# A hybrid decoder layer: interleaved output projection, grouped down product, weight loads issued from GpSimd

## The chip, the cores and the metric

The kernel runs on one core of one Trainium2 chip. The metric is the device time of one execution in microseconds, the median of several runs. Smaller is better. The engines are called as the profile calls them: PE (TensorE), DVE (VectorE), ACT (ScalarE), POOL (GpSimd), SP (SyncE, which only issues transfers here).

## The reference

One layer for 1024 prompt tokens and 8 x 8 decode tokens, 1088 in all, model width 1024, MLP width 4096. Two mixers (retention, and sliding-window attention with sinks) read one projection of the normed input; `concatenate([o_r, o_s])` below is their result. The part that the change touches starts behind them:

```python
    h = x + jnp.concatenate([o_r, o_s], axis=-1) @ w_out
    hf = rms_norm(h, norm_ffn_gain)
    h = h + jnp.square(jax.nn.relu(hf @ w_up)) @ w_down
    return h, new_ret, new_k, new_v
```

## The kernel before

All large products are fp32 in three passes: each operand is split into a rounded high part and the rest, and `mm3` issues high x high, low x high, high x low. A split (`halve`) is an ACT cast for the high part and a subtraction on DVE or POOL for the low part (`lo`).

The 1088 tokens are two halves s = 0, 1 of 544, each in two column blocks h of Q = 272. The stages follow each other:

- **Front**: input projection, retention and attention. Their results go to DRAM (`mr_hi_d` and so on) and come back as `mixa` (attention) and `mixr` (retention) for one half s at a time (`mix_load`).
- **Output projection**, `out_proj(s, m)` for eight blocks m of 128 output rows, 48 matmuls each. It loads and splits the block of w_out (`wo`), multiplies it by mixa and mixr, adds the residual x (`y`), stores the sum to DRAM (`y_d`), and keeps it times the norm's gain in `f` and its squares in `acc`. Half 0 is interleaved with the last retention blocks; half 1 follows with the eight PSUM banks of `psM`.
- **Operands**: up and down use a scheme with seven products instead of eight for a 2 x 2 block product. `operands(s, m)` forms the seven right-hand operands (`op0` to `op6`) as differences of `f` on POOL, and splits them (casts on ACT, `lo` on DVE).
- **Norm**, `norm(s)`: column sums of `acc` on PE (`psr`), scaling on DVE, a power on POOL (`rsqrt_inplace`), and then two transfers to DRAM and a broadcast load back give the factor `rsf` on all partitions. norm(0) is issued after m = 1 of half 1, norm(1) inside the first block of up.
- **Up**, 16 blocks `up(fp)`: the left operands `wu` are w_up's four quarters and three combinations of them that POOL adds up (`left`, `comb`), in the order PROD = (1, 2, 6, 5, 7, 4, 3), 48 / 2 = 24 matmuls each over both halves. The results are rectified, scaled by `rsf`, squared (`m`, `v`, `r`, `rt`), turned into the next product's operands by differences on POOL (`rt`) and stored to DRAM (`u_d`).
- **Down**, eight groups of two blocks of w_down: for each of seven products i the two blocks' left operands (`wd..a`, `wd..b`) and the stored operands (`ur`, split into `uh` and `ul`) are multiplied into eight PSUM banks (`psd`), and each bank is added to an accumulator `a` in SBUF. The stored y (`yt`) is added during groups 1 to 6.

Tile pools hand out buffers; whoever needs one waits until its last reader is done (`wa`, `wb`: four split weights each; `raw`: three raw weight halves). A scheduler decides the order of the instructions on each engine ahead of time, and every engine works its own list in order. All data transfers are issued from SP's list. `psM` and all of the last stages' buffers belong to the last four stages, so each stage's first loads wait for buffers of the one before.

## Time and profile before

| | |
|---|---|
| median of 3 runs | 1321.57 us (1320.02 to 1322.45) |
| the profiled execution | 1318.76 us, span 1317.0 us |
| busy share of the span | PE 93%, DVE 64%, POOL 53%, ACT 38% |
| mean granted TensorE clock | 0.966 |
| front and half 0 of the output projection | to about 518 us |
| half 1 | 518 to 598 us |
| up | 598 to 953 us |
| down | 953 to 1317 us |

A row of groups reads: line, engine, operation, written tile <- read tiles, shape, count, then busy time and the mean of one in ns, then the idle time of the engine before them and what ended it. A row of PE's waits reads: the waiting matmul, what it waited for, total us, how often, the longest. A row of a window gives for each engine its busy time and the number of instructions, then the granted clock (1.00 is full speed).

### The profile page before, as it was taken

Reading aid. Unit: us, or ns where it says so; the run is one execution under the profiler, and the core shown is the slowest. Engines: PE = TensorE matmul, PEld = TensorE weight load, DVE = VectorE, ACT = ScalarE, POOL = GpSimd, SP = SyncE. Lnnn points to the kernel's source line nnn. Section 1 sums busy time; section 2 is a strip of 40 time slices with the busy share of each in tenths; the row PEclk is TensorE's granted clock in tenths of the full one; section 3 lists DMA queues with packets and bytes.
Section 4 is the critical chain, followed back from the end, with each engine's and each line's share of the span. In section 5 each row is a group of like instructions: output and inputs, shape, how many; then the busy total and the mean of one; then the engine's idle time right before and its main releaser. Section 6 shows DMA issues by size and latency. Waiting matters only on the chain.

```text
span 1317.0 us, 24166 instructions
## 1 busy us (share of the span) xinstructions
PE 1227.8 (93%) x9581; PEld 1161.9 (88%) x9581; DVE 842.5 (64%) x1549; ACT 504.5 (38%) x1027; POOL 696.0 (53%) x542
## 2 busy tenths in 40 slices
PE   7989999999998698595999999999959999999998
PEld 5979877778978698595999999999959999999998
DVE  8736645543136567486666666767455888888886
ACT  5333334354213324153444344444444333333331
POOL 8325232222324423225566666656685887789761
PEclk9989999999999899698999999999989999999999
DMA  6211223324405855562243424243544445545434
GB/s 222 66 55 56 76 78 96 114 79 127 124 35 183 283 185 166 117 186 71 108 152 124 171 105 183 93 183 112 202 159 142 154 157 178 167 153 157 142 103 170
DMA packets 112778, 178.96 MB, mean 136 GB/s; under 512 B 14048, under 2 KB 82592, under 8 KB 112408
## 3 DMA queue, kind: packets, MB, share of 16 engines
q1 hardware_dynamic: 112663, 177.41, 41.1%
q8 instruction: 75, 1.23, 0.4%
q14 instruction: 40, 0.32, 0.1%
HBM read 119.31 MB, written 58.07 MB: 135 GB/s over the span
## 4 chain that ended last, share of the span: by engine, by line
PE 77%; DMA 8%; DVE 7%; POOL 5%; issue 1%; ACT 1%; SPq 0%; DVEq 0%; ACTq 0%; POOLq 0%
PE psd L181 7%; PE psd L179 7%; PE psd L180 7%; PE psx L179 5%; PE psx L181 5%; PE psx L180 5%; PE psf L181 3%; PE psf L179 3%; PE psf L180 3%; PE psz L181 2%; PE psz L179 2%; PE psz L180 2%; PE pst L179 2%; PE pst L180 2%; PE pst L181 2%; PE po L421 2%
## 5 line engine op out<-in xcount | busy, mean ns | idle before, releaser
L1045 DVE TENSOR_TENSOR a<-a,psd 128x272 f32<-128x272 f32 x416 | 162.4, 429 | 43.8 <-PE psd L181 43.3
L755 DVE TENSOR_TENSOR ul<-ur,uh 128x1088 fp32r<-128x1088 f32 (+1 forms) x57 | 108.5, 1908 | 25.9 <-ACT uh L754 23.7
L367 POOL TENSOR_TENSOR sp<-sp,ssp 128x1024 f32<-128x1024 f32 (+1 forms) x16 | 28.6, 1787 | 110.0 <-DVE ssp L366 110.0
L179 PE MATMUL psx<-op_1h,wu_w 128*128 128x272 f32 x256 | 75.0, 293 | 7.1 <-ACT m L974 7.1
L755 DVE TENSOR_TENSOR wu_w<-wu_s,wu_w 128x512 fp32r<-128x512 f32 x64 | 69.9, 1093 | 15.9 <-ACT wu_w L754 14.7
L179 PE MATMUL psx<-op_0h,wu_w 128*128 128x272 f32 x256 | 74.9, 292 | 0.0
L181 PE MATMUL psx<-op_1l,wu_w 128*128 128x272 f32 x256 | 74.7, 292 | 0.0
L181 PE MATMUL psx<-op_0l,wu_w 128*128 128x272 f32 x256 | 74.5, 291 | 0.0
L180 PE MATMUL psx<-op_1h,wu_w 128*128 128x272 f32 x256 | 74.3, 290 | 0.0
L180 PE MATMUL psx<-op_0h,wu_w 128*128 128x272 f32 x256 | 74.1, 289 | 0.0
L961 DVE SCALAR_TENSOR_TENSOR m<-m,rsf 128x272 f32<-128x272 f32 x96 | 61.8, 644 | 11.9 <-DMA rsf<-r_d 9.2
L754 ACT CAST uh<-ur 128x1088 fp32r<-128x1088 f32 (+1 forms) x57 | 61.8, 1087 | 9.0 <-PE psd L180 9.0
L181 PE MATMUL psf<-hnl,wqk_hi 128*128 128x384 f32 (+1 forms) x192 | 65.0, 339 | 0.0
L995 POOL TENSOR_TENSOR rt<-rt 128x272 f32<-128x272 f32 x64 | 64.3, 1014 | 1.2
L179 PE MATMUL psf<-hnh,wqk_hi 128*128 128x384 f32 (+1 forms) x192 | 64.9, 338 | 0.0
L180 PE MATMUL psf<-hnh,wqk_lo 128*128 128x384 f32 (+1 forms) x192 | 64.8, 338 | 0.0
L995 POOL TENSOR_TENSOR rt<-r,rt 128x272 f32<-128x272 f32 x32 | 31.7, 992 | 62.0 <-ACT r L962 62.0
L755 DVE TENSOR_TENSOR wu_w<-wu_r,wu_w 128x512 fp32r<-128x512 f32 x48 | 41.6, 868 | 27.5 <-ACT wu_w L754 27.5
L179 PEld LDWEIGHTS psx<-op_1h,wu_w 128*128 128x128 f32 x256 | 48.8, 191 | 7.3 <-ACT m L974 7.3
L956 DVE TENSOR_TENSOR m<-m,psz 128x272 f32<-128x272 f32 x64 | 28.0, 437 | 41.5 <-ACT m L974 26.6
L754 ACT CAST wu_w<-wu_s 128x512 fp32r<-128x512 f32 x64 | 39.8, 622 | 37.4 <-PE psy L181 30.5
L403 DVE SCALAR_TENSOR_TENSOR sp<-dtab,nsl,scp 128x256 f32<-128x256 f32 (+1 forms) x64 | 28.5, 459 | 37.4 <-PE scp L402 37.0
(511 smaller groups left out, 4902.8 us busy)
## 6 DMA issues: line engine op xcount, KB each, us to landing
u_d<-rt SPq DMA_DIRECT2D x32, 952.0 KB, 5.7
ur<-u_d SPq DMA_DIRECT2D x56, 544.0 KB, 4.0
wu_r<-in_w_up SPq DMA_DIRECT2D x32, 512.0 KB, 4.2
wo_raw<-in_w_out SPq DMA_DIRECT2D x16, 512.0 KB, 4.1
y<-in_xY SPq DMA_DIRECT2D x16, 272.0 KB, 3.0
y_d<-y SPq DMA_DIRECT2D x16, 272.0 KB, 2.4
yt<-y_d SPq DMA_DIRECT2D x16, 272.0 KB, 3.6
out_yT<-a SPq DMA_DIRECT2D x16, 272.0 KB, 2.2
```

What stands on the lines that cost most here:

```text
L179: nc.tensor.matmul(ps, lh, rh, start=first, stop=False, skip_group_check=more)
L180: nc.tensor.matmul(ps, ll, rh, start=False, stop=False, skip_group_check=more)
L181: nc.tensor.matmul(ps, lh, rl, start=False, stop=last, skip_group_check=more)
L367: nc.gpsimd.tensor_tensor(s, s, ss.unsqueeze(2).broadcast_to([P, 4, n]), ALU.mult)
L403: nc.vector.scalar_tensor_tensor(s[:, g, :], dtab[:, 256 - n :], nsl[:, c, kv, g : g + 1], pg, ALU.mult, ALU.add)
L421: nc.tensor.matmul(po[p_, :], vs[:, c - 1 + h, p_], pts[kv][:, h, :], start=h == halves[0], stop=h == 1)
L754: nc.scalar.copy(hi, src)
L755: lo_eng.tensor_tensor(lo, src, hi.bitcast(F32), ALU.subtract)
L956: nc.vector.tensor_tensor(t_, t_, bank_, ALU.add)
L961: nc.vector.scalar_tensor_tensor(t_, src, 0.0, rsf[:, s, h, :], ALU.max, ALU.mult)
L995: sub = lambda o_, p_, q_: nc.gpsimd.tensor_tensor(o_, p_, q_, ALU.subtract)
L1045: nc.vector.tensor_tensor(to, to, ps, ALU.add)
```

## The change

Four things are done, all behind the front:

1. **Output projection.** Each block is split into an `a` half (mixa) and an `r` half (mixr), and w_out is loaded as pairs of such halves. In half 1 the `a` halves of m = 0 to 3 come first, the `r` halves after them, then pairs m = 4, 5 and 6, 7. In half 0 the split weights are made one block ahead. `operands(0, ...)` are interleaved with half 1. The squares get a tile of their own.
2. **Norm.** The factors no longer pass through DRAM: PE broadcasts them with matmuls against the identity (`psn`), and ACT copies them into `rsf`. norm(0) moves behind m = 2, 3. The first two products' weights of up are split while the output projection ends.
3. **Down.** Five groups of 2, 4, 4, 4 and 2 blocks instead of eight of 2, so that fewer banks are emptied (448 become 280, 32 of them by ACT as before); the `lo` subtraction of `wd` moves from POOL to DVE. The y additions stand in groups 1 and 2.
4. **Transfers.** The raw loads of w_up and w_down, the loads of y and the stores `y_d` are issued from GpSimd.

```diff
     def rawload(src, name, tag="raw", pl=None):
-        raw = (pl or mw).tile([P, 1024], F32, tag=tag, name=name, bufs=3)
-        nc.sync.dma_start(raw, src)
+        raw = (pl or mw).tile([P, 1024], F32, tag=tag, name=name, bufs=9 if tag == "rawb" else 3)
+        nc.gpsimd.dma_start(raw, src)
         return raw
...
+    def wo_pair(s, m, half):
+
+        raw = mw.tile([P, 1024], F32, tag="raw", name=f"wo{half}{s}_{m}_raw", bufs=3)
+        c0 = 512 * (half == "a")
+        nc.sync.dma_start(
+            raw.rearrange("p (m n) -> p m n", m=2), a["w_out"][m : m + 2, :, c0 : c0 + 512].rearrange("m p n -> p m n")
+        )
+        for i in range(2):
+            yield wsplit(raw[:, i * 512 : i * 512 + 512], "wa", f"wo{half}{s}_{m + i}", nc.vector)
+
+    def out_half(s, half, ps, h, w, first, last):
+        for k in range(4):
+            lh, ll = (w[:, i, k * 128 : k * 128 + 128] for i in range(2))
+            mh, ml = (mix[s, half + x][:, k, h, :] for x in "hl")
+            mm3(ps, lh, ll, mh, ml, first and k == 0, last and k == 3)
+
+    def residual(s, m, pss):
         y = om.tile([P, 2, Q], F32, tag="y", name=f"y{s}_{m}", bufs=2)
-        nc.sync.dma_start(y.rearrange("p h n -> p (h n)"), a["xY"][:, s, m, :])
+        nc.gpsimd.dma_start(y.rearrange("p h n -> p (h n)"), a["xY"][:, s, m, :])
         for h in range(2):
...
-            nc.vector.tensor_tensor(y[:, h, :], ps, y[:, h, :], ALU.add)
+            nc.vector.tensor_tensor(y[:, h, :], pss[h], y[:, h, :], ALU.add)
         kk, k2 = m % 4, m // 4
-        nc.sync.dma_start(y_d[:, 2 * k2 : 2 * k2 + 2, kk, s, :], y)
+        nc.gpsimd.dma_start(y_d[:, 2 * k2 : 2 * k2 + 2, kk, s, :], y)
...
+    def out_parts(s, ms, half, psum, pss):
+
+        for m in ms:
+            if m % 2 == 0:
+                gen = wo_pair(s, m, half)
+            w = next(gen)
+            for h in range(2):
+                if half == "a":
+                    pss[m, h] = psum()
+                out_half(s, half, pss[m, h], h, w, half == "a", half == "r")
...
-        nc.vector.tensor_scalar(rf, ps[:, :5], 1.0 / 1024.0, EPS, ALU.mult, ALU.add)
-        rsqrt_inplace(rf, 5)
-        c0 = 2 * Q * s
-        nc.sync.dma_start(r_d[c0 : c0 + 512].rearrange("(t p) -> p t", p=128), rf[:, :4])
-        nc.sync.dma_start(r_d[c0 + 512 : c0 + 544].rearrange("(p t) -> p t", t=1), rf[96:128, 4:5])
-        nc.sync.dma_start(
-            rsf[:, s, :, :].rearrange("p h n -> p (h n)"), r_d[c0 : c0 + 544].unsqueeze(0).broadcast_to([P, 544])
-        )
...
+        nc.vector.tensor_scalar(rf, ps[:, :6], 1.0 / 1024.0, EPS, ALU.mult, ALU.add)
+        rsqrt_inplace(rf, 6)
+        for h in range(2):
+            pb = psM.tile([P, 512], F32, tag="b", name=f"psn{s}{h}")
+            for i, (c0, n) in enumerate(((0, 128), (128, 128), (256, 16))):
+                nc.tensor.matmul(
+                    pb[:, c0 : c0 + n], rf[:, 3 * h + i : 3 * h + i + 1].broadcast_to([P, 128]), ident[:, 128 - n :],
+                    start=True, stop=True,
+                )
+            nc.scalar.copy(rsf[:, s, h, :], pb[:, :Q])
...
+    out_parts(1, range(4), "a", late, pss)
+    for m in (2, 6, 3, 7):
+        operands(0, m)
+    mx0x.close()
+    operand_tiles(1)
+    mix_load(1, "r", ox.enter_context(pool("mxR", side="right")))
+    rest = [0, 4, 1, 5]
+    for ms in ((0, 1), (2, 3), (4, 5), (6, 7)):
+        if ms[0] > 3:
+            out_parts(1, ms, "a", late, pss)
+        out_parts(1, ms, "r", late, pss)
+        if ms == (6, 7):
+            gen0 = left(PROD, a["w_up"][0], "wu0", nc.vector, tags=("wa", "wa", "wb", "wb"))
+            ready = [next(gen0), next(gen0)]
+        for m in ms:
+            residual(1, m, [pss[m, h] for h in range(2)])
+            if rest:
+                operands(0, rest.pop(0))
+            operands(1, m)
+        if ms == (2, 3):
+            norm(0)
...
-    for g in range(8):
-        gens = [
-            left(DOWN, a["w_down"][2 * g + 1], f"wd{g}b", nc.gpsimd, "rawb", dn, "Sb", dn, ("wb",)),
-            left(DOWN, a["w_down"][2 * g], f"wd{g}a", nc.gpsimd, tags=("wa",)),
-        ]
+    for g, (f0, nf) in enumerate(((0, 2), (2, 4), (6, 4), (10, 4), (14, 2))):
+        gens = []
+        for f in range(nf):
+            own = ("rawb", dn, "Sb", dn) if f else ("raw", mw, "S", mid)
+            gens.append(left(DOWN, a["w_down"][f0 + f], f"wd{f0 + f}", nc.vector, *own, tags=("wb" if f % 2 else "wa",)))
```

How the lists of the engines move is shown at three places. The first is DVE at the end of half 0. Before, from the last block's weights on (`wo1_1` is block 1 of half 1, `op0_0l` a low part of half 0's operands; runs of such rows are cut short here):

```order
L755 TENSOR_TENSOR wo1_0_1_5398<-wo1_0_raw_5393,wo1_0_1_5398 128x512 [waits Activation_49]
L788 TENSOR_TENSOR y0_7_5213<-pso_5215,y0_7_5213 128x272 [waits DMAHW6_49,PE_49]
L802 TENSOR_TENSOR acc0_4589<-acc0_4589,y0_6_5146 128x544 [waits Activation_49]
L788 TENSOR_TENSOR y0_7_5213<-pso_5241,y0_7_5213 128x272 [waits PE_49]
L755 TENSOR_TENSOR op3_0l_5289<-f0_1_4654,op3_0h_5288 128x272 [waits Activation_49]
L755 TENSOR_TENSOR wo1_1_0_5467<-wo1_1_raw_5465,wo1_1_0_5467 128x512 [waits Activation_49]
L755 TENSOR_TENSOR op3_0l_5289<-f0_2_4816,op3_0h_5288 128x272 [waits Activation_49]
L796 TENSOR_SCALAR f0_7_5268<-y0_7_5213,c_g_ffn_103 128x544 [waits DVE_49]
L755 TENSOR_TENSOR wo1_1_1_5470<-wo1_1_raw_5465,wo1_1_1_5470 128x512 [waits Activation_49]
```

Changed:

```order
L756 TENSOR_TENSOR woa1_0_5305<-woa1_0_raw_5303,woa1_0_5305 128x512 [waits DMAHW7_49,Activation_49]
L756 TENSOR_TENSOR woa1_1_5334<-woa1_0_raw_5303,woa1_1_5334 128x512 [waits Activation_49]
L798 TENSOR_TENSOR y0_7_5269<-pso_5219,y0_7_5269 128x272 [waits DMASW5_49,DMASW4_49,PE_49]
L798 TENSOR_TENSOR y0_7_5269<-pso_5220,y0_7_5269 128x272 [waits PE_49]
L756 TENSOR_TENSOR woa1_2_5365<-woa1_2_raw_5363,woa1_2_5365 128x512 [waits DMAHW3_49,Activation_49]
L756 TENSOR_TENSOR woa1_3_5394<-woa1_2_raw_5363,woa1_3_5394 128x512 [waits Activation_49]
L756 TENSOR_TENSOR wor1_0_5486<-wor1_0_raw_5484,wor1_0_5486 128x512 [waits DMAHW6_49,Activation_49]
L756 TENSOR_TENSOR wor1_1_5513<-wor1_0_raw_5484,wor1_1_5513 128x512 [waits Activation_49]
```

The `a` weights of four blocks are ready around the last addition of half 0; the `r` weights of block 1 come seventeen DVE instructions after it. The second place is SP's list around mixr of half 1, before and changed:

```order
L764 DMA wo1_5_raw_5787<-in_w_out 128x1024 [waits DMAHW5_49,DVE_49]
L837 DMA r_d_126<-rst_166 128x4x1 [waits Pool_49]
L773 DMA mixrh1_5389<-mr_hi_d_130 128x4x544 [waits DMAHW7_49,PE_49]
L773 DMA mixrl1_5391<-mr_lo_d_131 128x4x544 [waits DMAHW0_49,DVE_49]
L838 DMA r_d_126<-rst_166 32x1 [waits DMAHW1_49]
```

```order
L782 DMA wor1_2_raw_5587<-in_w_out 128x2x512 [waits DMAHW1_49,DVE_49]
L782 DMA woa1_4_raw_5728<-in_w_out 128x2x512 [waits DMAHW3_49,DMAHW2_49,DVE_49]
L782 DMA wor1_4_raw_5788<-in_w_out 128x2x512 [waits DMAHW6_49,DVE_49]
L774 DMA mixrh1_5480<-mr_hi_d_130 128x4x544 [waits DMAHW5_49,DMAHW4_49,PE_49]
L774 DMA mixrl1_5482<-mr_lo_d_131 128x4x544 [waits DMAHW7_49,DMAHW0_49,DVE_49]
```

The norm's transfers are gone from around mixrh1, and a load that waits for DVE (the split of `wor1_1`, whose raw tile it takes over) stands ahead of it. The third place is POOL's list between up and down in the changed kernel (`rt15_1` is up's last result, `wd1` the second block of down, `wd2` the first of the next group):

```order
L1052 TENSOR_TENSOR rt15_1_9960<-rt15_1_9960 128x272 [waits Pool_49]
L957 TENSOR_TENSOR wd2_s6_10895<-wd2_s5_10893,wd2_r1_10744 128x512 [waits DMASW2_49,Pool_49]
L765 DMA wd1_r1_10223<-in_w_down 128x1024 [waits PE_49]
L765 DMA wd1_r2_10225<-in_w_down 128x1024 [waits PE_49]
L765 DMA wd3_r1_10751<-in_w_down 128x1024
L765 DMA wd5_r2_10767<-in_w_down 128x1024
L765 DMA wd7_r1_11722<-in_w_down 128x1024 [waits DMASW4_49]
L957 TENSOR_TENSOR wd1_s5_10308<-wd1_r2_10225 128x512 [waits DMASW5_49,PE_49]
L957 TENSOR_TENSOR wd1_s6_10310<-wd1_s5_10308,wd1_r1_10223 128x512 [waits PE_49,Pool_49]
```

The loads of wd1, which before stood in SP's list, come behind up's last differences and behind two operations for wd2.

More of the change, by code (lines that the diff above doesn't have):

```diff
@@ L2 @@
 from contextlib import ExitStack
+from itertools import chain
 import numpy as np
@@ L817, in operands @@
             put(B21, f[:, 0, :])
-            put(B22, f[:, 1, :])
             b12, t1 = fs[s, kk][:, 1, :], fs[s, kk][:, 0, :]
@@ L868, in hymba_layer, with out_early @@
     mx0 = mx0x.enter_context(pool("mx0", side="right"))
+    early = lambda: psA.tile([P, 512], F32, tag="mm", name="pso")[:, :Q]
+    def out_early(m):
+        if m % 2 == 0:
+            gens["a"], gens["r"] = (wo_pair(0, m, x) for x in "ar")
+            ahead.extend(next(gens[x]) for x in "ar")
+        wa_, wr_ = ahead
+        ahead.clear()
+        if m % 2 == 0:
+            ahead.extend(next(gens[x]) for x in "ar")
+        pss = [early() for h in range(2)]
+        for h in range(2):
+            out_half(0, "a", pss[h], h, wa_, True, False)
+            out_half(0, "r", pss[h], h, wr_, False, True)
+        residual(0, m, pss)
+    gens, ahead = {}, []
     mix_load(0, "a", mx0)
-    mix_load(1, "a", mxA)
     mix_block(4, *held[4])
     mix_load(0, "r", mx0)
-    early = lambda: psA.tile([P, 512], F32, tag="mm", name="pso")[:, :Q]
     for t in (5, 6, 7):
@@ L904, in operand_tiles @@
             ]
-    late = lambda: bank("pso")
-    operand_tiles(0)
-    for m in range(8):
-        operands(0, m)
-    mx0x.close()
-    operand_tiles(1)
-    mix_load(1, "r", ox.enter_context(pool("mxR", side="right")))
-    for m in range(8):
-        out_proj(1, m, late)
-        operands(1, m)
-        if m == 1:
-            norm(0)
-    ox.close()
-    mid = ctx.enter_context(pool("u", side="right"))
     def left(order, src, name, lo_eng, raw_tag="raw", raw_pool=None, s_tag="S", s_pool=None, tags=("wa", "wb")):
@@ L1004, in hymba_layer @@
     opx.close()
+    ux.close()
     dn = ctx.enter_context(pool("dn", side="left"))
@@ L1036, in hymba_layer @@
                     ps = banks[m, s]
-                    for f in range(2):
+                    for f in range(nf):
                         lh, ll = (ws[f][:, j, m * 128 : m * 128 + 128] for j in range(2))
-                        mm3(ps, lh, ll, uu[0][:, f, s, :], uu[1][:, f, s, :], first and f == 0, f == 1, not first)
+                        mm3(ps, lh, ll, uu[0][:, f, s, :], uu[1][:, f, s, :], first and f == 0, f == nf - 1, not first)
                     to = accs[q_][:, m, s, :]
```

71 lines of the change are left out of this document (36 added, 35 removed).

## The prediction, made before the changed kernel was run

> **What bounds the kernel now.** I read the busy shares and the 40 slices first. TensorE is busy nearly all the time, and where its slices or its clock dip, the stages meet.
>
> ```profile
> PE 1227.8 (93%) x9581; PEld 1161.9 (88%) x9581; DVE 842.5 (64%) x1549; ACT 504.5 (38%) x1027; POOL 696.0 (53%) x542
> PE   7989999999998698595999999999959999999998
> PEclk9989999999999899698999999999989999999999
> ```
>
> Then busy time by stretch: 518 to 598 is the second half of the output projection, 598 to 650 the start of the MLP's up product, 953 to 1000 the joint from up to down.
>
> ```profile
> core 0: us, PE busy (x) PEld busy (x) DVE busy (x) ACT busy (x) POOL busy (x), PEclk, DMA share, GB/s
> 518.00:598.00 80.00, 59.32 (x453) 58.17 (x451) 53.34 (x99) 29.67 (x68) 26.55 (x29) 0.83 0.52 135
> 598.00:625.00 27.00, 13.34 (x124) 12.88 (x124) 15.62 (x20) 9.02 (x20) 15.44 (x12) 0.78 0.32 78
> 625.00:650.00 25.00, 24.84 (x179) 24.84 (x180) 16.75 (x24) 10.49 (x24) 16.45 (x14) 0.90 0.30 116
> 650.00:953.00 303.00, 303.00 (x2403) 302.59 (x2401) 194.09 (x297) 131.68 (x299) 190.65 (x171) 1.00 0.39 144
> 953.00:985.00 32.00, 15.04 (x101) 14.37 (x101) 18.51 (x6) 14.14 (x31) 31.31 (x27) 0.84 0.51 179
> 985.00:1000.00 15.00, 14.48 (x105) 14.48 (x106) 3.76 (x5) 9.34 (x22) 5.47 (x4) 0.88 0.47 139
> 1000.00:1100.00 100.00, 100.00 (x806) 100.00 (x805) 81.47 (x153) 35.17 (x51) 76.44 (x50) 1.00 0.48 153
> ```
>
> Up runs at 303.00/2403 = 0.126 us a matmul, down at 100/806 = 0.124, both without a gap at full clock. What a stretch lost is its length less its matmuls at that rate, which counts idle time and the half-speed clock after it together: 518 to 598, 80 - 453 x 0.126 = **22.9**; 598 to 650, 52 - 303 x 0.126 = **13.8**; 953 to 1000, 47 - 206 x 0.124 = **21.4** us. The number of large matmuls does not change, so the change can earn these 58 us, little more, and lose whatever it puts in the way of 650 to 953 and 1000 to 1317. TensorE's own waits name the causes (total, times, longest):
>
> ```profile
> PE pso L179 <- DMA mixrh<-mr_hi_d: 11.9, 2, 10.3
> PE psd L181 <- DVE ul L755: 11.3, 1, 11.3
> PE pso L180 <- DVE wo L755: 10.7, 3, 6.1
> PE psx L179 <- ACT m L974: 7.1, 1, 7.1
> PE psy L179 <- ACT wu_w L754: 4.3, 1, 4.3
> PE pso L179 <- ACT wo L754: 3.9, 2, 3.7
> PE psd L179 <- ACT uh L754: 2.7, 1, 2.7
> PE psd L179 <- DVE a L1045: 2.6, 2, 1.6
> PE psy L180 <- DVE wu_w L755: 2.6, 1, 2.6
> ```
>
> The chain of waits (start, us, work) shows what lies behind the large ones:
>
> ```profile
> 457.42 5.73 DMA mixrh<-mr_hi_d
> ...
> 538.86 13.68 DMA mixrh<-mr_hi_d
> ...
> 607.47 1.56 POOL nsinks L133
> 609.47 9.47 DMA r_d<-nsinks
> 618.99 4.84 DMA rsf<-r_d
> ...
> 955.16 3.20 POOL rt L995 x3
> ...
> 971.32 14.15 DVE ul L755
> ```
>
> Both norms pass through DRAM. The first one's writes, of 4 bytes each, stood around the mixrh load, which took 13.68 us where the same load for the other half took 5.73; the second one's are 9.47 + 4.84 us of the start of up. These are the DMA answers for 536 to 556:
>
> ```profile
> mixrh<-mr_hi_d SPq DMA_DIRECT2D x1, 1088.0 KB, 13.7
> r_d<-rst SPq DMA_DIRECT2D x1, 2.0 KB, 8.1
> r_d<-rst SPq DMA_DIRECT2D x1, 0.1 KB, 15.3
> ```
>
> **Second half of the output projection: 14 us gained.** The 6.1 us and most of the other wo waits come from order: on VectorE the four wo1_0 and wo1_1 splits stood among the op splits. Now woa1_0 and woa1_1 are split before the first op, woa1_2 and woa1_3 right after the last residual add of the first half. TensorE can run the four a-blocks, 96 matmuls, 12.1 us, without mixrh. The mixrh load lost its r_d company, but in SyncE's queue it stands behind wor1_4's raw load, which needs a raw slot that the wor1_1 split frees. That split is 17 VectorE instructions after the last add of the first half; at the stretch's mean of 53.34/99 = 0.54 us they take 9.2. With two issues (0.33 and 0.57, rows under GpSimd's issues) and 5.73 for the load, mixrh is there at 15.8, so TensorE waits 3.7, not 10.3. New is norm(0) on TensorE's own queue: its broadcast matmuls stand ahead of the blocks m = 4 to 7 and wait for VectorE's scale and POOL's pow (1.56) behind other POOL work, about 3 us. With 2 for the half clock after these waits the stretch loses 8.7 where it lost 22.9: 14.2 gained. Ends: with the load at 13.68 it loses 17 (6 gained); with both waits at a third, 4 (19 gained). VectorE cannot be forgotten here: it has 53.34 us of the same work against 57 of TensorE's, so it is close behind.
>
> **Start of up: 7 us.** The products w1 and w2 are split ahead of the joint, which removes the 4.3 and 2.6 waits; the 7.1 behind the two DMAs becomes pow, an ACT copy and the queues, about 3. TensorE has 48 matmuls (6 us) between the last out-projection block and psr1, while VectorE finishes the last sum of squares; I add 2 for its lag and 1.5 for the clock: 6.5 where 13.8 was lost. Ends: 13 and 2.
>
> **First half: 2 us.** The look-ahead by one block takes the 3.7 us ACT wo wait; y's loads and stores on POOL's queue now stand ahead of the mixb splits there and wait for VectorE. I take 2, ends 4 and -3.
>
> **GpSimd's DMA issues.** No row shows one. 96 transfers move to it (32 w_up, 32 w_down, 32 y). Below, the issue costs 0.33 us as on SyncE; above, 1.56, the pow on 128x5 elements, nearly all fixed cost. I take 1.0, between them.
>
> ```profile
> 537.36 0.33 SPq L764 DMA_DIRECT2D wo_raw<-in_w_out  x1
> 538.86 0.57 SPq L773 DMA_DIRECT2D mixrh<-mr_hi_d  x1
> wu_r<-in_w_up SPq DMA_DIRECT2D x32, 512.0 KB, 4.2
> L754 ACT CAST wu_w<-wu_s 128x512 fp32r<-128x512 f32 x64 | 39.8, 622 | 37.4 <-PE psy L181 30.5
> ```
>
> In up POOL is busy 190.65 of 303, and each weight block has eight split buffers, 24 us of matmuls, ahead: nothing. The Trainium skill's page "DMA: Bandwidth & Descriptors" (Anatomy of one DMA) fits 2.0 us plus bytes/436e3 to a GpSimd transfer, 3.2 us for 512 KB; that would make the sum 1 us shorter than the 4.2 that I use. No run here shows it yet.
>
> **Joint from up to down: 1 us.** This is where I expect more and find little. The wd lo splits leave POOL, so the 2.4 us wd0b wait and half of POOL's burst go. But wd1, needed 3 us into down, is now loaded by POOL, whose queue first does the last rt differences (3.20 from 955.16, so to about 957.5), the combination wd2_s5, which waits for a load, one difference, and wd2_s6: about 960.8, for a block that is not needed for 42 us. Issue 1.0, landing 4.2, cast 0.6 (rows above): 966.6. TensorE starts at 953 + 2.7 = 955.7 as now and has 24 matmuls, to 958.7: 7.9 idle. Seven more issues follow, then the combinations wd1_s5 and s6 (to 971.3), then six more back to back. These rows on POOL run from one to the other without a gap while VectorE's ul needed 14.15 where one takes 1.64 on average (row under Down):
>
> ```profile
> 970.75 1.30 POOL L755 TENSOR_TENSOR wd0b_w<-wd0b_r,wd0b_w 128x512 fp32r<-128x512 f32 x1
> ...
> 983.06 1.25 POOL L932 TENSOR_TENSOR wd1b_s<-wd1b_r,wd1b_r 128x512 f32<-128x512 f32 x1
> ```
>
> So a VectorE instruction with two SBUF inputs gets through only when POOL pauses. wd1_w6's lo split then waits 6 x 1.25 = 7.5 us, of which TensorE feels 6.9. In all 2.7 + 7.9 + 6.9 + 3 for the clock = 20.5 where 21.4 was lost. Ends: 13.6 without the second wait (8 gained), 2.7 + 8.5 + 14.15 + 4 = 29 with issues at 1.56 and a wait like ul's (8 lost).
>
> **Down: nothing.** VectorE has 168 evictions fewer (416 to 248), but 112 lo splits more. For 100 us of TensorE, 806 matmuls, 8.4 products of four blocks:
>
> ```profile
> L1045 DVE TENSOR_TENSOR a<-a,psd 128x272 f32<-128x272 f32 x131 | 51.5, 430 | 13.4 <-PE psd L181 13.1
> L755 DVE TENSOR_TENSOR ul<-ur,uh 128x1088 fp32r<-128x1088 f32 x17 | 27.9, 1640 | 2.1 <-ACT uh L754 1.8
> L1053 DVE TENSOR_TENSOR a<-a,yt 128x544 f32<-128x544 f32 x5 | 4.4, 880 | 3.1 <-DMA yt<-y_d 3.1
> L755 DVE TENSOR_TENSOR wu_w<-wu_s,wu_w 128x512 fp32r<-128x512 f32 x64 | 69.9, 1093 | 15.9 <-ACT wu_w L754 14.7
> ```
>
> 67 evictions x 0.43 = 29, 17 ul x 1.64 = 28, 9.6 yt x 0.88 = 8.5, and 34 lo splits. Those took 1.093 in up, where POOL was busy 63%; in down POOL keeps 16 combinations of 1.25 in 83 us, 24%. At 0.8 they are 27, in all 92 of 100: TensorE remains the bound, with the 2.6 waits for a gone and others of that size come. Ends +2.6 and -10.
>
> **Sum:** 14.2 + 7.3 + 2 + 0.9 + 0 = 24.4 us off the profiled execution's 1318.76: 1294.4. The median, 1321.57, is 2.8 above it, so **1297**, with an own range of 1285 to 1310.
>
> **Rivals.** *VectorE becomes the bound in down* (slower). If a lo split costs on VectorE the 1.30 of the wd0b row on POOL, and each ul waits for one POOL instruction more (1.64 + 1.25), 100 us of TensorE need 29 + 49 + 44 + 8.5 = 130 of VectorE. Groups 1 to 3 last 250 us; half of that excess, 115 in 100, is 38 us: 1297 + 38 = **1335**. From 110 on it eats the 24.4. For it: 81.47 of 100 is busy already. Against: POOL loses 112 splits there, and with them most of what VectorE waits for. 15 in 100.
>
> *VectorE takes turns with POOL*: it waits for one POOL instruction, not for a burst. Then the second wait at the joint shrinks to 1.25 and its clock share goes, and so do the waits that I put in place of the 2.6: 8 + 2.6 less, **1286**. For it: the ul average of 1.64 in down, beside a POOL that was busy 76.44 of 100, leaves no room for long waits; against, the 14.15. The Trainium skill's page "SBUF — State Buffer" (SBUF: two separate sides) states this: the shared port pair is an exclusive lock held for one whole instruction. The 14.15 us row goes against a wait that short. 15 in 100.
>
> *All joints close*: every term at its better end, 19 + 13 + 4 + 8 + 2.6 = 47: **1275**. 10 in 100.
>
> *POOL's queue takes it back*: each y store there waits for an add, and each y load for the store two blocks earlier; operand differences stand behind. If the second half comes at its poor end (14 - 6 = 8 less) and first half and start of up half way to theirs (half of 5 + 5), 13 go: **1310**. 15 in 100.
>
> The forecast has 45. A difference within 0.2%, 2.6 us, is what cannot be told from no change; of the last rival's 15 I put 6 there, 2 beyond it and 7 below. So slower is 15 + 2 = 17, same 6, faster 77. Leaving out a tenth at each side, the range is 1272 to 1326.
>
> **What would show it.** The r_d and rsf rows gone after 500; mixrh's wait under 5 us; no wo wait over 2; a wait of psn for pow of about 3, twice; a psd wait for wd1's cast of some 8 us with POOL's wd2 rows ahead of the issue, and one for a wd1 lo split while POOL runs without a pause; VectorE near 92% in down and TensorE without gaps there. I am wrong if TensorE shows gaps in 1000 to 1250 that VectorE ends, or if mixrh still waits 10.

## The result and the profile after

The change makes the kernel slower, by 0.7%. Four runs took 1331.42 us in the median (1329.36 to 1331.53), the kernel before on the same chip 1322.01 (1320.02 to 1323.84): ratio **1.0068**, 95% interval 1.0052 to 1.0083. The forecast was 1297, range 1272 to 1326. The profiled execution took 1331.53 us, its span 1329.7, its mean granted clock 0.969. A second set of runs, on another chip, gave 1.0049 [1.0031, 1.0068]. Chips differ by up to half a per cent (the kernel before took 1322.01 us here and 1328.22 on the chip of e1), so below the ratios compare each kernel with runs of the kernel before on its own chip.

Busy shares, and TensorE's 40 slices, after:

```profile
PE 1236.5 (93%) x9621; PEld 1167.1 (88%) x9621; DVE 856.0 (64%) x1492; ACT 497.1 (37%) x1030; POOL 581.5 (44%) x526
PE   7979999999998699498999999999849999999998
```

POOL fell from 696 to 581 busy us and TensorE's share did not move. The dip at the joint is still there (slices 29 and 30). The stretches that answer to those before, by the same columns:

```profile
core 0: us, PE busy (x) PEld busy (x) DVE busy (x) ACT busy (x) POOL busy (x), PEclk, DMA share, GB/s
600.00:652.00 52.00, 46.70 (x358) 46.29 (x348) 37.41 (x52) 22.59 (x52) 34.26 (x34) 0.90 0.27 96
652.00:963.70 311.70, 297.45 (x2314) 295.00 (x2312) 201.31 (x288) 120.16 (x287) 201.34 (x191) 0.99 0.37 133
963.70:1010.00 46.30, 25.64 (x177) 25.21 (x178) 20.02 (x17) 20.43 (x45) 31.66 (x33) 0.82 0.72 252
```

By the prediction's measure (length less matmuls at 0.126, in down 0.124), the start of up lost 52 - 358 x 0.126 = 6.9 us where 13.8 was lost. But the rest of up, which had lost nothing, lost 311.7 - 2314 x 0.126 = 20 us. The joint lost 46.3 - 177 x 0.124 = 24.4 where it was 21.4.

With the first and the last matmul of each product in the trace as bounds, all kernels of this study compare in one table (us; the last column is the ratio to the kernel before on the same chip). Each row is one profiled execution, on one of several chips, and those of e2, e4, e8 and e11 took 2.7, 3.7, 6.2 and 2.7 us more than their kernel's median, that of before 2.8 less, so a difference of a few us between two rows needs its cause in the traces:

| kernel | half 1 | up | up's end to down's start | down | ratio |
|---|---|---|---|---|---|
| before | 76.4 | 358.4 | 2.7 | 357.5 | 1 |
| the change | 73.5 | 371.5 | 15.3 | 347.2 | 1.0068 |
| e1_wu_sp | 72.7 | 351.6 | 15.8 | 347.4 | 0.9885 |
| e2_tags | 75.5 | 377.7 | 14.9 | 348.2 | 1.0075 |
| e3_wo_pool | 72.7 | 373.1 | 15.4 | 347.5 | 1.0042 |
| e4_ur_act | 73.7 | 373.7 | 9.6 | 351.4 | 1.0003 |
| e5_wu_sp_tags | 73.9 | 352.0 | 14.2 | 345.0 | 0.9890 |
| e6_op_pool | 84.2 | 351.7 | 15.7 | 347.7 | 0.9991 |
| e7_joint | 72.8 | 351.7 | 9.6 | 348.6 | 0.9853 |
| e8_last_store_pool | 74.2 | 355.4 | 3.0 | 355.0 | 0.9859 |
| e9_loads_sp | 74.1 | 352.7 | 12.7 | 345.0 | 0.9879 |
| e10_all_sp | 75.8 | 352.8 | 12.7 | 345.4 | 0.9895 |
| e11_loads_sp_own | 72.6 | 356.6 | 3.6 | 345.8 | 0.9812 |

So the 12.8 us between the first two profiled executions come about as follows: half 1 starts 0.5 later and is 2.9 shorter, up is 13.1 longer (7 shorter at its start, 20 longer after it), the pause between up and down is 12.6 longer, down is 10.3 shorter, and what follows it 0.3 shorter.

TensorE's waits after (the waiting matmul, what it waited for, total us, times, longest):

```profile
PE psd L180 <- ACT uh L755: 15.3, 1, 15.3
PE pso L180 <- DMA mixrh<-mr_hi_d: 14.7, 1, 14.7
PE psx L180 <- ACT m L1031: 14.2, 8, 3.4
...
PE psd L180 <- ACT wd_w L755: 4.7, 1, 4.7
PE psn L861 <- POOL nsinks L134: 4.7, 1, 4.7
...
PE psn L861 <- POOL rst L134: 3.3, 1, 3.3
```

The waits that the change was to remove are gone or 0.6 us at most: the wo waits (10.7 and 3.9), the 4.3 and 2.6 for wu_w, the 11.3 for ul; the 7.1 behind the norm's transfers became the two for `psn`. Three large ones stand in their place (the one for mixrh, 11.9 before, grew).

**Up** first. ACT's idle time ahead of its rectifications in up, before (650 to 953) and after (652 to 963), last fields idle us and what ended it:

```profile
L962 ACT ACTIVATE rt<-m 128x272 f32<-128x272 f32 x59 | 24.6, 430 | 35.0 <-DMA u_d<-rt 28.8 <-DVE m L961 5.8
```

```profile
L1019 ACT ACTIVATE rt<-m 128x272 f32<-128x272 f32 x56 | 24.2, 431 | 122.0 <-DMA u_d<-rt 84.4 <-DVE m L1018 37.6
```

ACT writes `rt`, of which there are two buffers, so it waits until the buffer's last store to `u_d` has landed. That store waits for POOL's differences, and these wait for ACT's results. So the work of one block goes round a ring: ACT, POOL, the store, and ACT again. What stands behind the waiting ACT instruction, copies of `psx` among it, is what TensorE waits for (14.2 us in 8 waits; part of the rest of the 20 us goes with the granted clock, 0.99 over these 311.7 us where it was 1.00). Before, ACT waited 28.8 us there, and TensorE was busy without a gap from 650 to 953. Now the ring sets the pace: the median time from POOL's first difference of one block to that of the next (the period below) rose from 21.17 to 22.63 us. POOL's list in one such block after (start, us, work, and in brackets the idle time before it and what ended it):

```profile
767.48 3.35 POOL L1052 TENSOR_TENSOR rt<-rt 128x272 f32<-128x272 f32 x3
770.77 0.58 POOL L765 DMA_DIRECT2D wu_r<-in_w_up  x1
777.24 1.70 POOL L957 TENSOR_TENSOR wu_s<-wu_r 128x512 f32<-128x512 f32 x1 [5.90 <-DMA wu_r<-in_w_up]
...
784.20 0.91 POOL L1052 TENSOR_TENSOR rt<-r,rt 128x272 f32<-128x272 f32 x1 [0.33 <-ACT r L1019]
```

A load of w_up stands behind a block's last difference. POOL then stands still for 5.90 us until a load lands, and after its four combinations little is left before the next differences, which waited only 0.33 us for ACT. Before, POOL waited there for ACT, with its combinations done:

```profile
785.17 0.79 POOL L995 TENSOR_TENSOR rt<-r,rt 128x272 f32<-128x272 f32 x1 [3.96 <-ACT r L962]
```

**The pause at the joint.** SP's list and POOL's, after:

```profile
966.24 5.16 SPq L1057 DMA_DIRECT2D u_d<-rt  x2
971.49 1.96 SPq L1081 DMA_DIRECT2D ur<-u_d  x2
```

```profile
969.08 1.26 POOL L957 TENSOR_TENSOR wd_s<-wd_r 128x512 f32<-128x512 f32 x1 [0.73 <-DMA wd_r<-in_w_down]
970.29 0.76 POOL L1052 TENSOR_TENSOR rt<-rt 128x272 f32<-128x272 f32 x1
...
972.21 4.22 POOL L765 DMA_DIRECT2D wd_r<-in_w_down  x8
```

and SP's before:

```profile
945.43 1.97 SPq L1021 DMA_DIRECT2D ur<-u_d  x2
...
963.33 0.32 SPq L1000 DMA_DIRECT2D u_d<-rt  x1
```

Before, `ur0`, which needs only up's first two blocks, was issued 7.6 us ahead of up's end (953.0), and the last store to u_d came 18 us later. Now it stands behind that store. The store waits for POOL's last difference (970.29), which stands behind a combination for wd2 that waited 0.73 us for a load and took 1.26. So `ur0` was issued at 971.5, 7.8 us after up's end, and TensorE started down at 979.0.

**Half 1.** SP's list after:

```profile
538.39 0.37 SPq L782 DMA_DIRECT2D wor_raw<-in_w_out  x1
538.87 0.57 SPq L774 DMA_DIRECT2D mixrh<-mr_hi_d  x1
```

The prediction had the mixrh load landed 15.8 us into the stretch. It was issued only 20 us into it, right behind wor1_4, and took 7.5 to land.

### The profile page after: what moved, and what is told of

The parts are those of the page before. It is cut to its first block, busy times and chain, and to the rows that moved or that the text cites. A ratio compares the mean times of both kernels' runs of the same rounds, so it can differ in the third digit from the quotient of the medians.

```text
span 1329.7 us, 23999 instructions
## 1 busy us (share of the span) xinstructions
PE 1236.5 (93%) x9621; PEld 1167.1 (88%) x9621; DVE 856.0 (64%) x1492; ACT 497.1 (37%) x1030; POOL 581.5 (44%) x526
## 4 chain that ended last, share of the span: by engine, by line
PE 66%; DMA 10%; DVE 9%; POOL 8%; ACT 3%; issue 3%; SPq 0%; ACTq 0%; POOLq 0%; DVEq 0%
PE psd L181 8%; PE psd L182 8%; PE psd L180 8%; POOL rt L1052 6%; DMA u_d<-rt 5%; PE psf L182 3%; PE psf L180 3%; PE psf L181 3%; DVE wu_w L756 2%; PE pst L180 2%; PE pst L181 2%; PE po L422 2%; PE pst L182 2%; PE psx L180 2%; PE psx L182 2%
## 5 line engine op out<-in xcount | busy, mean ns | idle before, releaser
L180 PE MATMUL psd<-uh,wd_w 128*128 128x272 f32 x896 | 257.4, 290 | 20.0 <-ACT uh L755 15.3
L181 PE MATMUL psd<-uh,wd_w 128*128 128x272 f32 x896 | 260.4, 291 | 0.0
L182 PE MATMUL psd<-ul,wd_w 128*128 128x272 f32 x896 | 256.4, 289 | 0.6 <-DVE ul L756 0.6
L180 PEld LDWEIGHTS psd<-uh,wd_w 128*128 128x128 f32 x896 | 169.7, 190 | 20.5 <-ACT uh L755 15.5
L181 PEld LDWEIGHTS psd<-uh,wd_w 128*128 128x128 f32 x896 | 170.2, 190 | 0.0
L182 PEld LDWEIGHTS psd<-ul,wd_w 128*128 128x128 f32 x896 | 168.7, 189 | 0.9 <-DVE ul L756 0.9
L1100 DVE TENSOR_TENSOR a<-a,psd 128x272 f32<-128x272 f32 x248 | 101.7, 430 | 44.7 <-PE psd L182 44.7
L756 DVE TENSOR_TENSOR wu_w<-wu_s,wu_w 128x512 fp32r<-128x512 f32 x64 | 73.6, 1153 | 64.1 <-ACT wu_w L755 63.2
L756 DVE TENSOR_TENSOR ul<-ur,uh 128x1088 fp32r<-128x1088 f32 x56 | 87.3, 1585 | 21.4 <-ACT uh L755 21.3
L180 PE MATMUL psx<-op_0h,wu_w 128*128 128x272 f32 x256 | 75.8, 296 | 12.8 <-ACT m L1031 12.8
L755 ACT CAST wd_w<-wd_s 128x512 fp32r<-128x512 f32 x64 | 37.4, 619 | 112.1 <-PE psd L182 81.6
L1019 ACT ACTIVATE rt<-m 128x272 f32<-128x272 f32 x64 | 27.5, 431 | 130.3 <-DMA u_d<-rt 89.5
L755 ACT CAST uh<-ur 128x1088 fp32r<-128x1088 f32 x56 | 59.6, 1100 | 28.9 <-DMA ur<-u_d 19.9
```

The source lines that it names most:

```text
L180: nc.tensor.matmul(ps, lh, rh, start=first, stop=False, skip_group_check=more)
L181: nc.tensor.matmul(ps, ll, rh, start=False, stop=False, skip_group_check=more)
L182: nc.tensor.matmul(ps, lh, rl, start=False, stop=last, skip_group_check=more)
L755: nc.scalar.copy(hi, src)
L756: lo_eng.tensor_tensor(lo, src, hi.bitcast(F32), ALU.subtract)
L1019: nc.scalar.activation(dst, t_, AF.Square)
```

## The experiments

Three questions were open: which part of the change closed the ring in up, why the joint lost more, and why half 1 gained 2.9 and not 14. For up there were two theories: the w_up loads in POOL's list, or the new rotation of the split buffers (`tags`), the order of which (`wa`, `wa`, `wb`, `wb` where it was `wa`, `wb`) is also part of the change. With both of them ACT's list differs too: before, a block's last two copies of `psx` stand ahead of its second write to `rt`, and in the change that write stands between them or ahead of both, block by block in turn.

### e1_wu_sp: the w_up loads back on SP

```diff
-        nc.gpsimd.dma_start(raw, src)
+        (nc.sync if name.startswith("wu") else nc.gpsimd).dma_start(raw, src)
```

> The changed kernel with w_up's raw loads issued from SyncE again; w_down's stay on GpSimd. In ScalarE's list this puts both m7 copies ahead of the second rt write, as before the change. In the changed kernel up took 370.0 us from its first to its last matmul (592.2 to 962.2) where 356.9 stood before, and ScalarE waited 84.4 us for u_d stores (28.8 before). Theory A (the order of one ScalarE instruction, which only follows from where the loads are issued): up back to 357 +- 2, the 14.2 us of waits of psx for ScalarE's m gone, time 1318. Theory B (the weight loads in GpSimd's list hold back its differences): the same here. Rival C (the longer start of up, the new weight rotation or the pools): up stays at 368 to 371, time 1329 to 1332.

Ratio **0.9885** [0.9871, 0.9900]: 1.1% faster than the kernel before. 240 us in the middle of up, before, after and in e1 (columns as in the stretches above):

```profile
660.00:900.00 240.00, 240.00 (x1905) 239.81 (x1904) 159.53 (x239) 104.71 (x236) 155.18 (x139) 1.00 0.38 141
```

```profile
660.00:900.00 240.00, 229.04 (x1790) 227.25 (x1789) 158.36 (x224) 94.88 (x227) 156.42 (x147) 0.99 0.37 134
```

```profile
660.00:900.00 240.00, 240.00 (x1906) 240.00 (x1905) 156.44 (x238) 103.96 (x239) 150.49 (x136) 1.00 0.41 143
```

The change has 116 matmuls fewer than e1 in these 240 us, 14.6 us of work, and with the loads back on SP the period is 21.19 again. The whole of up is 351.6, 6.8 less than before: that is the start of up, for which 7.3 had been predicted. But in e1's trace the steady blocks have ACT's order of before, too (both copies ahead of the second write to `rt`), so e1 alone does not tell the loads from the order.

### e2_tags: only the old rotation of the split buffers in up

```diff
-        gen = chain(ready, gen0) if fp == 0 else left(
-            PROD, a["w_up"][fp], f"wu{fp}", nc.vector, tags=("wa", "wa", "wb", "wb"))
+        gen = chain(ready, gen0) if fp == 0 else left(PROD, a["w_up"][fp], f"wu{fp}", nc.vector)
```

> The changed kernel with up's split weights alternating between the two buffer groups again (wa, wb) from the second block on; all loads stay on GpSimd. ScalarE's list has both m7 copies ahead of the second rt write here too. Theory A (ScalarE's order): up at 357 to 360 although GpSimd issues the loads, time 1318 to 1321. Theory B (the loads in GpSimd's list themselves): up stays near 370, time 1331. Rival C (the weight rotation itself): as A here, but then e1 stays at 1331.

Ratio 1.0075 [1.0058, 1.0091], period 22.72, up 377.7. In ACT's list both copies of `psx` now stand ahead of the write again, as in the kernel before, and the ring is as slow as in the change. So neither the rotation nor ACT's order is the cause.

### e5_wu_sp_tags: both

The edits of e1 and e2 together.

> The changed kernel with w_up's loads on SyncE (as e1) and the weight rotation of before (as e2). With the rotation alone up kept its waits for ScalarE's m (19.4 us, 22.72 us a block). Theory (what closes the loop from rt's differences over the store of u_d back to rt is GpSimd's list with the loads in it; the rotation does nothing): a period of 21.2, up at 352 to 355, time within 3 us of e1 (0.988 of before). Rival (the rotation is what slows up and e1 was saved by ScalarE's order alone): the waits for m come back, up over 360.

0.9890 [0.9875, 0.9904], up 352.0, period 21.19: nothing beside e1. e2 and e5 differ in the place of the w_up loads alone, and ACT's order is that of before in the steady blocks of both. The middle of up in e2, then in e5:

```profile
660.00:900.00 240.00, 225.79 (x1748) 223.58 (x1747) 149.69 (x217) 89.17 (x217) 149.75 (x146) 0.99 0.37 135
```

```profile
660.00:900.00 240.00, 240.00 (x1905) 240.00 (x1905) 156.87 (x237) 105.72 (x239) 154.87 (x138) 1.00 0.40 149
```

With this the first question is settled: the w_up loads in POOL's list cost the 20 us. Which link of the ring pays was not tried apart and stays open. In the change POOL's differences end 0.5 us later after a block's first `r` than in e1, and the time from its second store to the next block's `r` is 13.75 against 12.78. POOL's standing still for a load is not the loss by itself: from 660 to 930 e1 stood still for w_up's loads for 51.2 us and the change for 40.1, yet e1's differences waited 27.4 us for ACT's `r` in that time and the change's only 5.7.

### e3_wo_pool: mixr no longer behind wor1_4

The later w_out pairs of half 1 are issued from POOL, so that in SP's list nothing that waits for a split stands ahead of `mixrh`.

```diff
-        nc.sync.dma_start(
+        (nc.gpsimd if s and m > 3 else nc.sync).dma_start(
```

> The changed kernel with the raw w_out loads of blocks 4 to 7 of half 1 issued from GpSimd, so that no load that waits for VectorE stands ahead of mixrh in SyncE's list. Theory (that place is what holds mixrh): mixrh is issued at the end of half 0, near 519, and not at 538.87; the wait of 14.7 us falls under 4, half 1 shortens by 8 to 11, time 1320 to 1323. Rival (VectorE bounds half 1, busy 58.9 of 80 us): the wait moves to VectorE's splits of wor and adds, and half 1 shortens by under 4 us, time 1327 to 1331.

1.0042 [1.0027, 1.0057], as the rival had it. The wait for mixrh is gone, and half 1 is only 0.8 us shorter. Other waits took its place in e3:

```profile
PE pso L181 <- DVE wor L756: 6.3, 2, 3.8
...
PE pso L182 <- DMA mixrl<-mr_lo_d: 4.2, 1, 4.2
```

```profile
519.34 0.57 SPq L774 DMA_DIRECT2D mixrh<-mr_hi_d  x1
541.79 0.57 SPq L774 DMA_DIRECT2D mixrl<-mr_lo_d  x1
```

`mixrl` takes over memory whose last readers are the low parts of half 0's operands (`op_0l`) on VectorE, and VectorE does them in between everything else. This is the change itself in the 28 us after TensorE has finished half 0:

```profile
519.00:534.00 15.00, 12.59 (x97) 11.93 (x95) 15.00 (x21) 8.52 (x23) 11.58 (x14) 1.00 0.22 74
534.00:547.00 13.00, 0.45 (x2) 0.48 (x3) 7.68 (x15) 2.17 (x5) 2.90 (x3) 0.53 0.65 222
```

VectorE is busy 15.00 of the first 15: both the `wor` splits and mixrl's buffer hang on it. So removing the queue's part uncovers VectorE's part, 10.5 us of waits where 14.7 were removed; the granted clock over half 1 was 0.84 in e3 and 0.86 in the change.

### e6_op_pool: take those low parts off VectorE

e1 and e3, and half 0's low parts computed on POOL:

```diff
-            halve(ops[i][s][0][:, kk, :], ops[i][s][1][:, kk, :], src, nc.vector)
+            halve(ops[i][s][0][:, kk, :], ops[i][s][1][:, kk, :], src, nc.gpsimd if s == 0 else nc.vector)
```

> As e1, with the loads of blocks 4 to 7 of half 1 on GpSimd (as e3, which took mixrh's 14.7 us wait away and won 0.8 us in half 1) and the low parts of half 0's operands subtracted on GpSimd, which takes about 28 instructions of 0.5 to 0.65 us from VectorE. Theory (VectorE bounds half 1, so the stretch stayed at 72.7 us): half 1 shortens by 8 to 14 us, to 59 to 65, time 1297 to 1303 where e1 has 1311 (0.980 of before). Rival (GpSimd's list, with y's transfers and the differences, bounds half 1): half 1 stays at 70 or grows.

0.9991 [0.9977, 1.0006], so 1.1% worse than e1, most of it in half 1 (84.2 us): the rival. POOL did the low parts later than VectorE had; mixrl, which waited 24.3 us in SP's list for POOL's `op_0l`, was issued at 553.88, and TensorE waited for it:

```profile
PE pso L182 <- DMA mixrl<-mr_lo_d: 19.6, 1, 19.6
```

And VectorE's other splits in half 1 became slower (mean ns of one), in the change 1116 and 753, in e6 1750 and 1327:

```profile
L756 DVE TENSOR_TENSOR woa<-woa_raw,woa 128x512 fp32r<-128x512 f32 x6 | 6.7, 1116 | 2.1 <-ACT woa L755 2.1
...
L756 DVE TENSOR_TENSOR wor<-wor_raw,wor 128x512 fp32r<-128x512 f32 x8 | 6.0, 753 | 2.3 <-ACT wor L755 2.3
```

```profile
L756 DVE TENSOR_TENSOR woa<-woa_raw,woa 128x512 fp32r<-128x512 f32 x6 | 10.5, 1750 | 6.6 <-ACT woa L755 6.6
L756 DVE TENSOR_TENSOR wor<-wor_raw,wor 128x512 fp32r<-128x512 f32 x8 | 10.4, 1327 | 2.8 <-ACT wor L755 2.8
```

POOL was busy 54.58 of 84 us there, 34.62 of 73.3 in the change. Part of the work that went from VectorE to POOL came back as time on VectorE. The Trainium skill's page "SBUF — State Buffer" (SBUF: two separate sides) describes this as an exclusive lock on a shared port pair, held for a whole instruction; the direction of these rows agrees, the lock itself is not to be seen in them.

### e4_ur_act: ur0 out of SP's list

```diff
-                nc.sync.dma_start(ur[:, f : f + 2], u_d[(f0 + f) // 2][:, :, :, RIGHT[i], :])
+                eng = nc.scalar if g == 0 and i in (1, 6) else nc.sync
+                eng.dma_start(ur[:, f : f + 2], u_d[(f0 + f) // 2][:, :, :, RIGHT[i], :])
```

> The changed kernel with the loads of the first two stored operands of down's first group (ur0) issued from ScalarE, not behind the last u_d store in SyncE's list. Theory (SyncE's order behind GpSimd's late difference): they are issued at about 966, not at 971.5; the 15.3 us wait for uh falls to 7 to 9, wd1's split becomes the next wait, and the time falls by 4 to 7, to 1324 to 1327. Rival (the nine raw weight loads that GpSimd issues at once fill the transfer bandwidth and hold ur): the load lands as late as now, time 1330 to 1332.

1.0003 [0.9989, 1.0017]; the pause is 9.6 us instead of 15.3, and down 4.2 longer. The place in SP's list is part of the pause. The rest: in ACT's list the issue stands behind up's last rectification, at 968.98, still 1.6 us after up's end.

### e0_after_again and e7_joint

The change again, beside e5 to e7:

> The changed kernel itself, to compare the others with it on the same chip. All theories: 1.0068 of the time before, up at a period of 22.65 us a block.

1.0049 [1.0031, 1.0068], up 372.5, pause 15.7: as the first time. Then e7: e1, e4, and buffers of its own for wd2's weights, so that POOL's last differences of up don't stand behind combinations that wait:

```diff
-            own = ("rawb", dn, "Sb", dn) if f else ("raw", mw, "S", mid)
+            own = ("rawb", dn, "Sb", dn) if f or g == 1 else ("raw", mw, "S", mid)
```

> As e1, with the first block of down's second group (wd2) in the buffers of the others, so that GpSimd does up's last differences and wd1's loads ahead of it, and with ur0's two loads issued from ScalarE (as e4). Theory (the joint is lost to the order in which GpSimd and SyncE work off their lists): from up's last matmul to down's first 7 to 9 us instead of 15.8, no wait for wd1's split over 2, time 9 to 12 us under e1, 0.980 of before. Rival (the transfers' bandwidth: nine loads of 512 KB at once): the first wait falls, but the wait for wd1 grows by as much, time within 3 us of e1.

0.9853 [0.9838, 0.9867]. It beats e1 by 0.3%, 4 us (e5, on the same chip, by 4.7), where 9 to 12 were expected. The pause is 9.6 as in e4, and 4.3 of wait for wd1's cast remain: the first load of the next group (now wd6) took wd2's place in POOL's list, with a combination that waited 1.86 us in front of the last difference. Moving one waiting instruction away had let the next one move up.

### e8_last_store_pool: clear SP's list instead

e1 and the buffers of e7; `ur0` stays on SP, and the stores of up's last block are issued from POOL, which computes them.

```diff
-                    nc.sync.dma_start(u_d[fp // 2][:, fp % 2, s, :, :], r)
+                    (nc.gpsimd if fp > 14 else nc.sync).dma_start(u_d[fp // 2][:, fp % 2, s, :, :], r)
```

> w_up on SyncE and the first block of down's second group in its own buffers (as in e7_joint), but instead of moving ur0 to ScalarE's list, the stores of up's last block are issued from GpSimd, which computes them; nothing in SyncE's list then stands ahead of ur0. Theory, every load of the joint is late because of what stands ahead of it in a list: TensorE's first wait shrinks from 9.6 to about 3, but wd1's loads still stand behind up's last differences in GpSimd's list, now behind two stores as well, so the wait for wd1's cast grows from 4.3 to about 10 and the time stays where e7_joint was, ratio 0.984 to 0.986. Rival, only ur0 mattered: the wait for wd1 stays near 4 and the ratio falls to about 0.981.

0.9859 [0.9842, 0.9876], the theory's 0.984 to 0.986. Both waits are as it had them (3 and 10):

```profile
PE psd L180 <- ACT wd_w L755: 10.6, 1, 10.6
...
PE psd L180 <- ACT uh L755: 3.1, 1, 3.1
```

`ur0` was on time. wd1, still in POOL's list, was not, and what one wait lost the other took, as the theory of the lists had said.

### e9_loads_sp and e10_all_sp: every weight load on SP

e8, with the w_down loads on SP too (`nc.sync.dma_start(raw, src)` for all); e10 has y's loads and stores there as well.

> As e8_last_store_pool, and the loads of w_down are issued from SyncE too, so GpSimd issues only y and the stores of up's last block. Theory of the lists: wd1 and ur0 are both issued before up ends, TensorE's two waits at the joint are 3 us or less each, up and down keep 351 and 347 us, and the ratio is about 0.978. Rival, the bandwidth at the joint is what decides (about 400 GB/s were moved there, nine or ten weight halves and ur0): the same bytes still have to come, the waits only change their name and keep 10 us together, ratio 0.984 or more.

0.9879 [0.9865, 0.9894]: the theory's 0.978 is missed, and the rival's "0.984 or more" holds, with the pause back at 12.7 us. But its cause is not bandwidth. SP's list in e9:

```profile
931.54 2.44 SPq L1057 DMA_DIRECT2D u_d<-rt  x2
946.82 1.28 SPq L765 DMA_DIRECT2D wd_r<-in_w_down  x3
948.15 1.33 SPq L1081 DMA_DIRECT2D ur<-u_d  x2
```

For 13 us SP issued nothing, and from 938 to 946 the DMA engines were busy for 1% of the time. The first of the three loads is one of wd6; it waited 12.7 us until VectorE had read its buffer for the last time, and wd1 and `ur0` stood behind it.

> As e9_loads_sp, with y and its stores on SyncE too: the change without its fourth part, but for the two stores of up's last block. Theory: y's place does nothing by itself, half 1 of the output projection stays at 73 +- 1 us and the time within 0.2% of e9_loads_sp. Rival: y on SyncE's list puts stores that wait for VectorE ahead of mixr, its wait of 15 us grows by 2 or more and half 1 takes 75 us or more; or GpSimd, free of the issues, lets VectorE run faster, and half 1 falls to 70 or below.

0.9895 [0.9877, 0.9913], within 0.2% of e9. Half 1 takes 75.8 us against 74.1, outside the theory's 73 +- 1 and over the rival's 75, but without the longer wait for mixrh that the rival named (14.2 where it was 15.6). y's place does little.

### e11_loads_sp_own: the same without that one waiting load

```diff
-            own = ("rawb", dn, "Sb", dn) if f or g == 1 else ("raw", mw, "S", mid)
+            own = ("rawb", dn, "Sb", dn) if f or g else ("raw", mw, "S", mid)
```

> As e9_loads_sp, where the load that stood still in SyncE's list was one of w_down's sixth block (first of the third group), which waits for a raw buffer of up and was issued only when up ended, with wd1 and ur0 behind it. Here the first block of every later group has its own buffers, so this load comes later in the list. Theory of the lists: wd1 and ur0 are issued some 10 us before up ends, TensorE's first wait falls from 12.7 to 4 or less and the wait for wd1's cast stays 3 or less, ratio 0.979 to 0.981. Rival, bandwidth: what comes at the joint is ten weight halves and two ur, 6.3 MB, 15 us at 400 GB/s; with the issues earlier the waits go over to wd1 and the lo splits, 10 us stay, and the ratio is 0.986 or more.

**0.9812** [0.9795, 0.9828], 1302.51 us where the kernel before took 1326.83 on that chip: the best kernel of the study, 1.9% faster than before. The theory had 0.979 to 0.981, bandwidth 0.986 or more. SP's list now:

```profile
937.08 1.64 SPq L765 DMA_DIRECT2D wd_r<-in_w_down  x2
944.77 2.99 SPq L1081 DMA_DIRECT2D ur<-u_d  x2
```

Both come ahead of up's end (950.4), the pause is 3.6 us, there is no wait for wd1, and down takes 345.8. The edit moved the first block of three groups to other buffers, and with wd6's load out of the way the pause is 9 us shorter. Up's last block became 5 us longer than in e1, with a wait of 3.1 for `m` in it; its cause was not looked for. In half 1 mixrh's wait of 15.5 is left.

That e11 ends at the ratio that was forecast for the change (1297 to 1321.57 is 0.981) is luck: half 1 gains 3.8 us where 14.2 were forecast, and from up's end to down's end it gains 10.8 where 0.9 was.

## Why the prediction was wrong, step by step

**Start of up, 7.3 gained: right.** 6.9 us lost where 6.5 were predicted, the two r_d and rsf transfers gone. The two waits for the norm's power on POOL were 3.3 and 4.7, not 3 each.

**GpSimd's DMA issues in up, for which the prediction put "nothing" into the sum: wrong, and the largest miss, 20 us.** The issue itself was dearer in the prediction than on the chip (1.0 us assumed):

```profile
L765 POOL DMA_DIRECT2D wu_r<-in_w_up x32 | 18.3, 573 | 22.4 <-DVE wu_w L756 17.6 <-DVE rst L856 2.4 <-DVE woa L756 1.8
L765 POOL DMA_DIRECT2D wd_r<-in_w_down x32 | 17.5, 550 | 41.3 <-DVE wd_w L756 35.4 <-DMA wd_r<-in_w_down 3.5 <-DVE wu_w L756 2.0
```

The cover was looked for in the wrong place: POOL's busy share (190.65 of 303) and the split buffers ahead of TensorE. Neither tells what stands behind the load in POOL's list, and when that is needed. The prediction asked this at the joint and not in up, where it named no ring at all; the row for `rt` before, with 28.8 us of waiting for u_d, was there to be read. In its place the runs showed a period of 22.6 us where 21.2 is possible, and that it goes with the place of these loads alone (e2 against e5). The landing took 4.1 us, near the 4.2 that the prediction took from SP's row, so its size did not decide. The fit on the Trainium skill's page "DMA: Bandwidth & Descriptors" (Anatomy of one DMA) gives an estimate of 3.2; the 4.1 is 0.9 more.

**Joint, 1 gained: 3 lost.** wd1 late behind wd2's rows was right in kind, a wait of 4.7 where 7.9 was predicted (one step of that sum is 0.9 off: 955.16 + 3.20 is 958.4, not 957.5). What failed is "TensorE starts at 953 + 2.7 = 955.7 as now": the operand's buffer was free, but its load had moved in SP's list behind the store that waits for POOL (with nothing ahead of it there, in e8, TensorE waited 3.1). The pause was 15.3. The third part, 6.9 for a split on VectorE while POOL runs without a pause, did not come: POOL itself stood waiting for its late loads (3.53 us of them from 976.4 on).

**Second half of the output projection, 14.2 gained: 2.9.** The terms are those of the prediction, in the wrong size: mixrh's wait was 14.7, not 3.7, which alone is the miss of 11. Half 0's last addition on VectorE came at 523.7, 4.8 us after TensorE's end, where none was counted; the 17 instructions took 14 us, not 9.2, 0.83 each where the mean over the whole stretch (0.54) was taken; the load landed in 7.5, not 5.73. "VectorE cannot be forgotten here" was the better reading: with the queue's part gone, in e3, waits for VectorE's work held half 1 at 72.7 us. e6, which took work from VectorE, did not get below that, because POOL did it later still; a half 1 that neither holds was not found.

**First half, 2 gained: 0.5 lost**, within its ends of 4 and -3.

**Down, nothing: right.** From 1010 to 1250 TensorE has no gap. Busy times there (columns as above), and VectorE's rows:

```profile
1010.00:1250.00 240.00, 240.00 (x1910) 240.00 (x1909) 198.08 (x304) 86.51 (x125) 80.00 (x64) 1.00 0.48 157
```

```profile
L1100 DVE TENSOR_TENSOR a<-a,psd 128x272 f32<-128x272 f32 x168 | 68.4, 429 | 26.9 <-PE psd L182 26.9
L756 DVE TENSOR_TENSOR ul<-ur,uh 128x1088 fp32r<-128x1088 f32 x41 | 65.3, 1626 | 0.0
L756 DVE TENSOR_TENSOR wd_w<-wd_s,wd_w 128x512 fp32r<-128x512 f32 x47 | 37.2, 810 | 4.8 <-ACT wd_w L755 4.8
```

The lo splits took 0.81 (0.8 predicted), ul 1.63 (1.64). VectorE's durations add up to 213 of 240 us, 89% against 92; as neighbours overlap, its busy share is 83%. The 10.3 us by which down is shorter are those by which its start is later: from up's end to down's end it is 360.2 before and 362.5 after.

**The rivals.** None of the four was it. VectorE as the bound in down and its taking turns with POOL both speak of contention that the trace does not show there. "POOL's queue takes it back" was nearest, but it put the loss in the output projection, and its price (13) was less than what up alone lost. The error lies in a rival that was not written: a load on a compute engine's list as part of up's ring.

## What to carry to other kernels

To move a transfer to a compute engine's list, don't price its issue: write down, for a steady block, what stands behind it in that list, what that work waits for, and whether the result comes back to the same engine; if it closes a ring, compare the ring's length with the block's time on the bound engine. For a transfer at a joint, the buffer being free is half of the answer; the other half is the first instruction ahead of it in its list that can wait. And a mean duration over a stretch need not be the duration in the piece that matters (0.54 and 0.83 here).

## What was not expected of the hardware

- An instruction that issues a 512 KB load took 0.55 to 0.57 us on POOL and 0.33 on SP, and w_up's loads landed about equally fast (medians of 4.1 and 4.2 us, issue to landing, in the change and before; in e2, between 660 and 900, POOL's took 7.1). What cost the 20 us here is the list, not the issue.
- The same VectorE subtraction on 128x272 took 0.43 or about 1.0 us in half 1, and on 128x512 between 0.68 and 2.56. It goes with what POOL did beside it: between 518 and 542, those of 0.43 had at most 0.28 us of a POOL instruction beside them, those of about 1.0 had 0.70 or more.
- The wait of 14.15 us of one VectorE instruction beside an unbroken run of POOL, which the prediction feared, did not come back in down: after 1010 no VectorE instruction took over 2.4 us. But two splits in up (at 629 and 718) took 6.1 each, beside an unbroken run of differences of some 0.77 us each on POOL.
